# A two-layer decoder trunk: every fourth weight chunk gets its low part from an accumulating DMA instead of VectorE

## The chip, the cores and the metric

The kernel runs on one core of one Trainium2 chip. The metric is the device time of one execution in microseconds. Two runs of the kernel before took 2312.23 and 2313.69 us, median 2312.96. The engines are called as in the profile: PE is TensorE's matmul, PEld its weight load, DVE VectorE, ACT ScalarE, POOL GpSimd, SP SyncE, which here only issues DMAs.

## The reference

A sequence of 256 tokens with 2048 features in float32 passes two layers. Each layer is a token mixer, a layer norm of `ALPHA * x + mixer(x)`, a gated feed-forward net with a short causal convolution, and a layer norm again. Layer 0 mixes by a gated linear recurrence (HGRN2), layer 1 by causal spatial gating (gMLP).

```python
def hgrn2_mixer(x, w_in, norm_g, w_out, lb):      # layer 0
    q, f, i, g = split(x @ w_in, 4)               # 2048 -> 4 x 2048
    ...                                           # recurrence over the tokens, 16 heads
    return (rms_norm(o) * norm_g * silu(g)) @ w_out

def chunked_gmlp(x, w_in, ln_g, ln_b, w_s, b_s, w_out):   # layer 1
    u, v = split(gelu(x @ w_in), 2)               # 2048 -> 2 x 2048
    ...                                           # v normed, mixed over tokens in chunks of 128
    return (u * gate) @ w_out

def conv_ffn(x, w_up, conv_w, conv_b, w_down):    # both layers
    a, b = split(x @ w_up, 2)                     # 2048 -> 2 x 5632
    a = causal_conv3(a, conv_w) + conv_b
    return (silu(a) * b) @ w_down                 # 5632 -> 2048

for layer in range(2):
    h = layer_norm(ALPHA * h + mixer[layer](h))
    h = layer_norm(ALPHA * h + conv_ffn(h))
```

Nearly all the work is in the products with weights. There are 392 blocks of 512 x 512 weights, each read once from HBM.

## The kernel before, in words

**Exact sums of two parts.** [...] The kernel keeps float32 accuracy by writing each operand as hi + lo, where hi is the value rounded to float32r and lo is what is left, and computes hi*hi + hi*lo + lo*hi. Activations X and Y are kept so for all 256 tokens. Weights are split as they arrive.

**Chunks.** A chunk is a 512 x 512 block of a weight matrix, [128, 4, 512] on chip, 1 MiB. `plan` lists all chunks in the order in which the products take them; `want` appends, with `extra=True` for six that use buffers of a pool of their own. `fetch` issues the DMA of the next chunk into a `raw` tile, on SP's queue. `convert` makes the tiles `hi` (named whi in the profile) and `lo` (wlo): in two pieces of 1024 columns, ACT copies raw to hi (L83), which rounds it, and DVE subtracts hi from raw into lo (L84). `chunk` is called by a product when it takes a chunk; it first calls `ahead(AHEAD)`, with AHEAD = 3, so that the fetch and the conversion of the next two chunks stand in the program ahead of the products of this one. raw, hi and lo have three buffers each (pool `wp`, `bufs=3`).

**Products.** In `block_b` the weights are stationary and the output has the features on the partitions: a block of 512 output features takes four chunks, each with 16 pairs of matmuls, L149 (hi times both parts of the activations) and L156 (lo times their high part). In `block_a` the activations are stationary (L113 hi, L114 lo, L115 hi): each chunk has 24 matmuls. Both need the low part in their first two instructions of a chunk. PE runs the chunks one after another in the order of the plan.

**Stages.** HGRN2: four groups of three `block_b`, one `block_a` and the recurrence, then the output product. FFN: the features go in groups of 3, 4 and 4 blocks of 512, each block two `block_b` (up) and, after each group, four `block_a` (down). gMLP: four `block_a` for v, four `block_b` for u with the gating, four `block_a` out. Then the FFN of layer 1.

**Order.** The instructions are recorded in program order and a scheduler orders them on each engine's queue by readiness as it reckons it; each engine then works its queue in order. On a queue an instruction that waits holds up what stands behind it. POOL's queue in the kernel before holds constants and, later, broadcasts: rows of layer-norm vectors (`g`, `b`, `gb`, `bb`, L314) and gMLP's biases and mixing weights (`bs` L685, `wsT` L655). `residual` applies a layer norm's gain and bias to z, ordered behind the last L84 recorded (`self.last_lo`).

Of the kernel before, what the change touches and what calls it, by code (L numbers as in the profile page):

```python
# [8 lines left out]
F32 = mybir.dt.float32  # L9
F32R = mybir.dt.float32r  # L10
U32 = mybir.dt.uint32
AF = mybir.ActivationFunctionType
ALU = mybir.AluOpType
# [20 lines left out]


class Trunk:
    """Activations that feed products are kept as an exact sum of two float32r parts,
    feature on the partition, [P, k, part, token]; weights are split the same way as
    they arrive, and a product is hi*hi + hi*lo + lo*hi."""

    def __init__(self, ctx, tc, a):
        self.tc = tc
        self.nc = nc = tc.nc
        self.a = a
        self.ctx = ctx
        ent = ctx.enter_context
        self.cp = ent(tc.tile_pool(name="cp", bufs=1))
        self.wp = ent(tc.tile_pool(name="wp", bufs=3))
        self.acc = ent(tc.tile_pool(name="acc", bufs=6, space=PSUM))
        self.misc = ent(tc.tile_pool(name="misc", bufs=2, space=PSUM))  # L50
        cp = self.cp
        self.X = cp.tile([P, NK, 2, S], F32R, name="X")
        self.Y = cp.tile([P, NK, 2, S], F32R, name="Y")
        self.z = cp.tile([P, 2, D], F32, name="z")
        self.small = ent(tc.tile_pool(name="small", bufs=2))
        self.plan = []
        self.issued = 0
        self.taken = 0
        self.ready = []

    # ---------------------------------------------------------------- weights
    def want(self, w, k0, c0, extra=False):
        self.plan.append((w, k0, c0, extra))

# [10 lines left out]
    def convert(self, raw, extra, pieces=2):  # L75
        nc = self.nc
        pool = self.xp if extra else self.wp
        hi = pool.tile([P, CK, NB], F32R, tag="hi", name="whi")
        lo = pool.tile([P, CK, NB], F32R, tag="lo", name="wlo")
        n = CK // pieces  # L80
        for i in range(0, CK, n):
            s = slice(i, i + n)
            nc.scalar.copy(hi[:, s, :], raw[:, s, :])  # L83
            self.last_lo = nc.vector.tensor_tensor(  # L84
                lo[:, s, :], raw[:, s, :], hi[:, s, :].bitcast(F32), ALU.subtract
            )
        self.ready.append((hi, lo))
# [8 lines left out]
        self.taken += 1  # L96
        return self.ready.pop(0)

    # ---------------------------------------------------------------- products
    def block_a(self, act, ka, w, k0, nch, c0, evac, staggered=False, halves=False):  # L100
        """out[token, c0:c0+NB]; act is stationary."""
        nc = self.nc
        ps = [self.acc.tile([P, NB], F32, tag="acc", name="pa") for _ in range(2)]
        n = [0, 0]

        def part(ch, ci, t):
            hi, lo = ch
            for kk in range(CK):
                k = ka + ci * CK + kk
                xh = act[:, k, 0, t * P : (t + 1) * P]  # L110
                xl = act[:, k, 1, t * P : (t + 1) * P]
                last = n[t] == nch * CK - 1
                nc.tensor.matmul(ps[t], xh, hi[:, kk, :], start=n[t] == 0, stop=False)  # L113
                nc.tensor.matmul(ps[t], xh, lo[:, kk, :], start=False, stop=False)  # L114
                nc.tensor.matmul(ps[t], xl, hi[:, kk, :], start=False, stop=last)  # L115
                n[t] += 1

        take = lambda ci: self.chunk(w, k0 + ci * CK, c0)
        first = max(0, nch - 4) if staggered else nch
        head = []  # L120
        if halves:
            head = [take(ci) for ci in range(min(3, nch))]
            for t in range(2):
                for ci, ch in enumerate(head):
                    part(ch, ci, t)
        for ci in range(len(head), first):
            ch = take(ci)
            for t in range(2):
                part(ch, ci, t)
        held = [take(ci) for ci in range(first, nch)]  # L130
        for t in range(2):
            for i, ch in enumerate(held):
                part(ch, first + i, t)
            if held:
                evac(t, ps[t])
        if not held:
            for t in range(2):
                evac(t, ps[t])

    def block_b(self, act, w, nch, c0, evac, halves=False):  # L140
        """out[c0 + feature, token] in four tiles, [P, main | rest, token]; the weights
        are stationary."""
        nc = self.nc
        ps = [self.acc.tile([P, 2, S], F32, tag="acc", name="pb") for _ in range(4)]
        last = nch * CK - 1
# [42 lines left out]
            evac(j, ps[j])  # L188

    def gather(self, pool, ps, out):  # L190
        """out = main + rest of a tile of block_b."""
        nc = self.nc
        r = pool.tile([P, S], F32, tag="rest", name="rest")
        nc.scalar.copy(r, ps[:, 1, :])  # L194
        nc.vector.tensor_tensor(out, ps[:, 0, :], r, ALU.add)

    def split(self, out, k, src):
        """out[:, k] = the two parts of src [P, token]."""
        nc = self.nc
        nc.scalar.copy(out[:, k, 0, :], src)  # L200
        nc.vector.tensor_tensor(
            out[:, k, 1, :], src, out[:, k, 0, :].bitcast(F32), ALU.subtract
        )

    # ---------------------------------------------------------------- constants
    def load_x(self, k0, n):
        x = self.a["x"][0].rearrange("(t p) d -> p t d", p=P)
        s = slice(k0 * P, (k0 + n) * P)
# [8 lines left out]
        nc.gpsimd.memset(self.eps[:, 1:2], RMS_EPS)  # L217

    def load_vectors(self, rows_sb):
        """Per-feature vectors as columns: feature k*P + p of row r at [p, base + k]."""  # L220
        nc, cp, a = self.nc, self.cp, self.a
        rows = []
        self.rows = []
# [45 lines left out]
        return self.cols[:, b + k : b + k + n]  # L269

    def bounds(self, h1):
        """lb = softmax over the rows of lb_logits, row 0, and 1 - lb."""
        nc, cp = self.nc, self.cp
        t = h1.tile([P, 6, NK], F32, tag="sg", name="lbt")
        m, e, rest, tot = t[:, 0, :], t[:, 1:4, :], t[:, 4, :], t[:, 5, :]
# [9 lines left out]
        nc.vector.tensor_tensor(self.lb[:, 0, :], e[:, 0, :], tot, ALU.mult)  # L285
        nc.vector.tensor_tensor(self.lb[:, 1, :], rest, tot, ALU.mult)

    # ---------------------------------------------------------------- layouts
    def turn(self, t, k0, n=4, g=None, b=None):
        """X[:, k0 : k0 + n, :, half t] from the columns of z[half t], with x -> g*x + b."""  # L290
        nc = self.nc
        ps = self.misc.tile([P, n, P], F32, tag="m", name="pt")
        for j in range(n):
# [14 lines left out]
            self.X[:, k0 : k0 + n, 1, s], src, hi.bitcast(F32), ALU.subtract  # L308
        )

    # ---------------------------------------------------------------- layer norm
    def broadcast(self, pool, ap, c, tag, **kw):
        r = pool.tile([P, NB], F32, tag=tag, name=tag, **kw)
        self.nc.gpsimd.dma_start(  # L314
# [10 lines left out]
        return mv  # L325

    def norm(self, name, l, store=None):
        """Layer norm of z, half by half as its last product arrives. With store, the
        result goes there; without, it goes to X, and z holds it once residual() has run."""
        nc = self.nc  # L330
        g, b = self.a[name + "_g"][l], self.a[name + "_b"][l]
        self.ln = ExitStack()
# [38 lines left out]
            self.ln.close()  # L371

    def add_z(self, c, first=False, last=False):
        """evac of block_a: z[:, t, NB columns c] gains the product, the first time as
        ALPHA * z + product."""
        nc = self.nc

        def evac(t, ps):
            with self.tc.high_priority() if last else nullcontext():
                step(t, ps)  # L380

        def step(t, ps):
            zz = self.z[:, t, c * NB : (c + 1) * NB]
            if first:
                nc.vector.scalar_tensor_tensor(zz, zz, ALPHA, ps, ALU.mult, ALU.add)
            else:
                nc.vector.tensor_tensor(zz, zz, ps, ALU.add)  # L387
            if last:
                nc.vector.bn_stats(self.stats[t][:, c, :], zz)
                if c == 3:  # L390
                    self.after_stats(t)

        return evac

    # ---------------------------------------------------------------- HGRN2
    def plan_hgrn(self):
        w, wo = self.a["hg_w_in"][0], self.a["hg_w_out"][0]
        for g in range(4):
# [7 lines left out]
            self.want(wo, 3 * CK, c * NB, c == 3)  # L406

    def masks(self):
        """mask[b][s, (group, i, r)] = 1 where row s lies in segment i of that group of four
        segments of b rows."""  # L410
        nc, cp = self.nc, self.cp
        self.mask = {}
        for b in LEVELS:
# [98 lines left out]
                self.split(self.Y, h, y.rearrange("p t n -> p (t n)"))  # L512

    def mix(self, q, f, k1, v, sc, o, ss, lp, h1):
        """Two heads. The decay between s < t is a product of forget gates; it is taken as
        (gates from s to the end of its segment) * (gates of the segments between) *
        (gates from the start of t's segment), at the one level of a division of the tokens
        by four at which s and t part. Q and K carry the outer two."""
        nc = self.nc
        flat = lambda x: x.rearrange("p h n -> p (h n)")  # L520
        own = lambda th: slice((th % 2 * 2 + th // 2) * P, (th % 2 * 2 + th // 2 + 1) * P)
# [95 lines left out]
        self.staggered_pass(self.Y, 12, wo, 12)  # L617

    def staggered_pass(self, act, ka, w, k0):
        """The last CK k-tiles of all four column blocks, half t = 0 first."""  # L620
        nc = self.nc
        ev = [self.add_z(c, last=True) for c in range(4)]
        held = [self.chunk(w, k0, c * NB) for c in range(4)]
# [9 lines left out]
                    nc.tensor.matmul(ps, xl, hi[:, kk, :], start=False, stop=kk == CK - 1)  # L633
                ev[c](t, ps)

    # ---------------------------------------------------------------- gMLP
    def plan_gmlp(self):
        w, wo = self.a["sg_w_in"][0], self.a["sg_w_out"][0]
        for part in (1, 0):
# [84 lines left out]
            self.block_a(self.Y, 0, a["sg_w_out"][0], 0, 4, c * NB,  # L724
                         self.add_z(c, first=True, last=True), staggered=c == 3)

    # ---------------------------------------------------------------- ConvFFN
    def plan_ffn(self, l):
        up, down = self.a["ffn_w_up"][l], self.a["ffn_w_down"][l]
        m = 0  # L730
# [125 lines left out]
```

## Time and profile before

| what | value |
|---|---|
| median of two runs | 2312.96 us (2312.23 to 2313.69) |
| span of the profiled execution | 2310.0 us |
| granted PE clock, mean | 0.998 |
| PE busy | 2287.9 us, 99% |
| DVE busy | 1499.2 us, 65% |
| ACT busy | 1090.2 us, 47% |
| POOL busy | 43.3 us, 2% |
| HBM read | 425.98 MB, 185 GB/s over the span |

The profile is of one execution; its span is from the first instruction to the last, and 3 us lie between it and the median of the runs. A group's row gives the line, the engine, the operation, the tiles written and read, the shapes, the count, then the busy time and the mean duration of one in ns, then the idle time of the engine just ahead and what ended it. A row of the timeline gives the start, the duration of what is merged in it, the engine and the operation, and in brackets the idle time before it. Matmuls are pipelined and their ends modelled.

### The profile page before, as it was taken

Reading aid. Unit: us, or ns where it says so; the run is one execution under the profiler, and the core shown is the slowest. Engines: PE = TensorE matmul, PEld = TensorE weight load, DVE = VectorE, ACT = ScalarE, POOL = GpSimd, SP = SyncE. Lnnn points to the kernel's source line nnn. Section 1 sums busy time; section 2 is a strip of 40 time slices with the busy share of each in tenths; the row PEclk is TensorE's granted clock in tenths of the full one; section 3 lists DMA queues with packets and bytes.
Section 4 is the critical chain, followed back from the end, with each engine's and each line's share of the span. In section 5 each row is a group of like instructions: output and inputs, shape, how many; then the busy total and the mean of one; then the engine's idle time right before and its main releaser. Section 6 shows DMA issues by size and latency. Waiting matters only on the chain.

```text
span 2310.0 us, 30477 instructions
## 1 busy us (share of the span) xinstructions
PE 2287.9 (99%) x12141; PEld 1956.5 (85%) x12141; DVE 1499.2 (65%) x2407; ACT 1090.2 (47%) x1642; POOL 43.3 (2%) x86
## 2 busy tenths in 40 slices
PE   8999999999999999999999999999999999999998
PEld 7888888888888888888888888888888888888886
DVE  5868786857765666456665776566765566466656
ACT  5565555536443444334443645445443444344442
POOL 2000000000000000000000000000000000000000
PEclk9999999999999999999999999999999999999999
DMA  7454535464466555555555676655565555555553
GB/s 257 129 185 137 187 134 185 146 234 158 170 214 218 188 183 182 200 182 187 191 189 182 201 223 192 214 181 178 189 228 182 193 183 189 194 189 183 182 198 112
DMA packets 214046, 430.05 MB, mean 186 GB/s; under 512 B 7544, under 2 KB 8336, under 8 KB 213904
## 3 DMA queue, kind: packets, MB, share of 16 engines
q1 hardware_dynamic: 209536, 415.26, 53.2%
q0 software_dynamic: 4368, 12.85, 1.9%
q8 instruction: 95, 1.56, 0.3%
q14 instruction: 47, 0.39, 0.0%
HBM read 425.98 MB, written 2.10 MB: 185 GB/s over the span
## 4 chain that ended last, share of the span: by engine, by line
PE 96%; DVE 2%; DMA 1%; ACT 0%; SPq 0%; issue 0%; DVEq 0%; ACTq 0%
PE pb L149 38%; PE pb L156 19%; PE pa L115 12%; PE pa L114 12%; PE pa L113 12%; PE pl L544 1%; DMA z<-in_x_dram 1%; DVE wlo L84 0%; PE pt L295 0%; DVE scores L553 0%; PE pg L710 0%; PE pa L632 0%; PE pa L633 0%; PE pa L631 0%; PE pl L577 0%; DVE K L559 0%
## 5 line engine op out<-in xcount | busy, mean ns | idle before, releaser
L84 DVE TENSOR_TENSOR wlo<-raw,whi 128x1024 fp32r<-128x1024 f32 (+1 forms) x786 | 929.4, 1218 | 683.5 <-ACT whi L83 675.6
L149 PE MATMUL pb<-X,whi 128*128 128x512 f32 (+1 forms) x3960 | 1348.8, 391 | 1.9 <-DVE X L307 1.9
L83 ACT CAST whi<-raw 128x1024 fp32r<-128x1024 f32 (+1 forms) x786 | 789.5, 1047 | 911.9 <-PE pb L149 435.3
L156 PE MATMUL pb<-X,wlo 128*128 128x256 f32 x3840 | 1054.5, 282 | 0.0
L149 PEld LDWEIGHTS pb<-X,whi 128*128 128x128 f32 x3960 | 726.5, 188 | 166.9 <-DVE X L307 2.4
L156 PEld LDWEIGHTS pb<-X,wlo 128*128 128x128 f32 x3840 | 713.1, 188 | 4.9
L115 PE MATMUL pa<-whi,Y 128*128 128x512 f32 x928 | 365.1, 393 | 0.0
L114 PE MATMUL pa<-wlo,Y 128*128 128x512 f32 x928 | 364.6, 393 | 0.0
L113 PE MATMUL pa<-whi,Y 128*128 128x512 f32 x928 | 361.3, 389 | 0.0
L114 PEld LDWEIGHTS pa<-wlo,Y 128*128 128x128 f32 x928 | 174.3, 188 | 39.6
L113 PEld LDWEIGHTS pa<-whi,Y 128*128 128x128 f32 x928 | 174.2, 188 | 38.8
L115 PEld LDWEIGHTS pa<-whi,Y 128*128 128x128 f32 x928 | 174.5, 188 | 35.3
L194 ACT COPY rest<-pb 128x256 f32<-128x256 f32 x240 | 87.3, 369 | 115.6 <-PE pb L149 112.3
L115 PE MATMUL pa<-whi,X 128*128 128x512 f32 x256 | 100.7, 393 | 0.0
L113 PE MATMUL pa<-whi,X 128*128 128x512 f32 x256 | 100.3, 392 | 0.0
L114 PE MATMUL pa<-wlo,X 128*128 128x512 f32 x256 | 100.2, 392 | 0.0
L761 DVE SCALAR_TENSOR_TENSOR act<-a,cols,act 128x254 f32<-128x254 f32 (+1 forms) x176 | 73.1, 477 | 0.0
L114 PEld LDWEIGHTS pa<-wlo,X 128*128 128x128 f32 x256 | 48.1, 188 | 10.8
L115 PEld LDWEIGHTS pa<-whi,X 128*128 128x128 f32 x256 | 48.1, 188 | 10.2
L113 PEld LDWEIGHTS pa<-whi,X 128*128 128x128 f32 x256 | 48.1, 188 | 10.0
L387 DVE TENSOR_TENSOR z<-z,pa 128x512 f32<-128x512 f32 x40 | 27.4, 684 | 34.3 <-PE pa L115 30.1
L553 DVE COPY_PREDICATED scores<-mask,pl 128x192 f32<-128x192 uint32 (+2 forms) x144 | 40.9, 354 | 2.0 <-PE pl L544 1.8
(161 smaller groups left out, 1082.0 us busy)
## 6 DMA issues: line engine op xcount, KB each, us to landing
raw<-in_ffn_w_up_dram SPq DMA_DIRECT2D x176, 1024.0 KB, 4.9
raw<-in_ffn_w_down_dram SPq DMA_DIRECT2D x88, 1024.0 KB, 5.1
raw<-in_hg_w_in_dram SPq DMA_DIRECT2D x63, 1024.0 KB, 5.1
raw<-in_sg_w_in_dram SPq DMA_DIRECT2D x32, 1024.0 KB, 5.5
raw<-in_hg_w_out_dram SPq DMA_DIRECT2D x16, 1024.0 KB, 5.1
raw<-in_sg_w_out_dram SPq DMA_DIRECT2D x16, 1024.0 KB, 5.1
g<-in_ln_g_dram POOLq DMA_DIRECT2D x16, 256.0 KB, 5.9
b<-in_ln_b_dram POOLq DMA_DIRECT2D x16, 256.0 KB, 8.7
```

The lines of the kernel that those rows point to most:

```text
L83: nc.scalar.copy(hi[:, s, :], raw[:, s, :])
L84: self.last_lo = nc.vector.tensor_tensor(lo[:, s, :], raw[:, s, :], hi[:, s, :].bitcast(F32), ALU.subtract)
L113: nc.tensor.matmul(ps[t], xh, hi[:, kk, :], start=n[t] == 0, stop=False)
L114: nc.tensor.matmul(ps[t], xh, lo[:, kk, :], start=False, stop=False)
L115: nc.tensor.matmul(ps[t], xl, hi[:, kk, :], start=False, stop=last)
L149: nc.tensor.matmul(ps[j][:, :, s], ch[0][:, k % CK, c], act[:, k, :, s], start=start and k == 0, stop=k == last, skip_group_check=halves,)
L156: nc.tensor.matmul(ps[j][:, 1, :], ch[1][:, k % CK, c], act[:, k, 0, :], start=False, stop=False, skip_group_check=halves,)
L194: nc.scalar.copy(r, ps[:, 1, :])
L387: nc.vector.tensor_tensor(zz, zz, ps, ALU.add)
L544: nc.tensor.matmul(pl[:, h, :], K[:, own(2 * t + h)], W[:, 2 * h + t, :], start=True, stop=True)
L553: nc.vector.copy_predicated(dst, mk.unsqueeze(1).to_broadcast([P, 2, P // 4 // b, w]), src)
L761: nc.vector.scalar_tensor_tensor(cv[:, d:], x[:, : S - d], self.c(("cw", l, 2 - d), f), cv[:, d:], ALU.mult, ALU.add,)
```

## The change

A counter in `convert` numbers the chunks in the order in which they are converted. From chunk 16 on, every fourth that isn't one of the extra ones is converted in another way: ACT copies raw to hi in one piece of 2048 columns, ACT writes -hi to lo, and a DMA issued by POOL adds raw onto lo. The result is the same, raw - hi. The other chunks keep the two pieces on ACT and DVE. `self.last_lo` is set by these alone. Docstrings and comment lines are emptied, so that line numbers after `convert` are 8 higher (L83 and L84 of other chunks are now L91 and L92).

```diff
@@ __init__
         self.taken = 0
+        self.formed = 0
         self.ready = []
@@ convert
         hi = pool.tile([P, CK, NB], F32R, tag="hi", name="whi")
         lo = pool.tile([P, CK, NB], F32R, tag="lo", name="wlo")
+        self.formed += 1
+        if self.formed > 12 and self.formed % 4 == 0 and not extra:
+            nc.scalar.copy(hi, raw)
+            nc.scalar.activation(lo, hi.bitcast(F32), AF.Copy, scale=-1.0)
+            nc.gpsimd.dma_start(lo, raw, accum_op=ALU.add)
+            self.ready.append((hi, lo))
+            return
         n = CK // pieces
...
```

ACT's queue in the FFN of layer 0, at the end of one feature block and the beginning of the next. Before (L83 is the cast to hi, L194 and L200 evacuate and split a product, L765 is the silu):

```order
L83 CAST whi<-raw 128x1024 x2
L200 CAST Y<-b 128x256 x2
L83 CAST whi<-raw 128x1024 x6
L194 COPY rest<-pb 128x256 x4
L83 CAST whi<-raw 128x1024
```

The same place with the change (lines 8 higher but for the new L83 and L84):

```order
L91 CAST whi<-raw 128x1024 x2
L208 CAST Y<-b 128x256 x2
L83 CAST whi<-raw 128x2048
L84 ACTIVATE wlo<-whi 128x2048
L91 CAST whi<-raw 128x1024 x4
L202 COPY rest<-pb 128x256 x4
L91 CAST whi<-raw 128x1024
```

Of three chunks cast in a row, the first now has one cast of double width, and the negation stands right behind it, ahead of the casts of the next two.

POOL's queue from the last blocks of gMLP's gating to its output product. Before (bs are biases, g and b the vectors of the next layer norm):

```order
L685 DMA bs<-in_sg_b_s_dram 128x512 x3
L314 DMA g_12413<-in_ln_g_dram 128x512
L314 DMA g_12415<-in_ln_g_dram 128x512
L314 DMA g_12417<-in_ln_g_dram 128x512
L314 DMA g_12419<-in_ln_g_dram 128x512
L314 DMA b_12421<-in_ln_b_dram 128x512
```

With the change (L85 is the accumulating DMA; the one ahead of the g rows is chunk 244's, the first behind the b rows chunk 248's):

```order
L85 DMA wlo<-raw 128x2048
L693 DMA bs<-in_sg_b_s_dram 128x512
L85 DMA wlo<-raw 128x2048
L322 DMA g_12358<-in_ln_g_dram 128x512
L322 DMA g_12360<-in_ln_g_dram 128x512
L322 DMA g_12362<-in_ln_g_dram 128x512
L322 DMA g_12364<-in_ln_g_dram 128x512
L322 DMA b_12366<-in_ln_b_dram 128x512
L322 DMA b_12368<-in_ln_b_dram 128x512
L322 DMA b_12370<-in_ln_b_dram 128x512
L322 DMA b_12372<-in_ln_b_dram 128x512
L85 DMA wlo<-raw 128x2048 x8
```

The broadcasts, which stood alone on this queue, now have accumulating DMAs between them, and the eight of the layer norm stand together ahead of chunk 248's.

## The prediction

> **What bounds the kernel now.** I read the page first: busy time, then the chain that ended last and the costliest groups.
>
> ```profile
> span 2310.0 us, 30477 instructions
> PE 2287.9 (99%) x12141; PEld 1956.5 (85%) x12141; DVE 1499.2 (65%) x2407; ACT 1090.2 (47%) x1642; POOL 43.3 (2%) x86
> ...
> PE 96%; DVE 2%; DMA 1%; ACT 0%; SPq 0%; issue 0%; DVEq 0%; ACTq 0%
> ...
> L84 DVE TENSOR_TENSOR wlo<-raw,whi 128x1024 fp32r<-128x1024 f32 (+1 forms) x786 | 929.4, 1218 | 683.5 <-ACT whi L83 675.6
> ...
> L83 ACT CAST whi<-raw 128x1024 fp32r<-128x1024 f32 (+1 forms) x786 | 789.5, 1047 | 911.9 <-PE pb L149 435.3
> ```
>
> TensorE is the bound and carries 96% of the chain. VectorE, which the change relieves, is on 2% of it and spends 683.5 us idle just ahead of L84, waiting for the high part. The windows view tells how much of TensorE's time could be won (columns: length, PE busy, PEld, DVE, ACT, POOL, granted clock, DMA share, GB/s), and the list of waits says what PE waited for.
>
> ```profile
> core 0: us, PE busy (x) PEld busy (x) DVE busy (x) ACT busy (x) POOL busy (x), PEclk, DMA share, GB/s
> ...
> 20.00:2290.00 2270.00, 2266.80 (x12041) 1939.25 (x12040) 1475.98 (x2371) 1078.82 (x1623) 27.07 (x50) 1.00 0.55 186
> 2290.00:2310.00 20.00, 9.85 (x43) 7.70 (x41) 13.08 (x23) 0.59 (x2) 0.00 (x0) 0.81 0.28 105
> ```
> ```profile
> PE pt L295 <- DMA z<-in_x_dram: 8.8, 4, 3.9
> PE pb L149 <- DVE X L307: 1.9, 2, 1.1
> PE pv L264 <- DVE cols L265: 0.5, 1, 0.5
> ```
>
> Between 20 and 2290 us PE is idle for 2270.00 - 2266.80 = 3.2 us, and no wait of PE names a weight tile. So the weights always come in time, and taking work off VectorE can win some 3 us at most. The question is whether a low part made by DMA still comes in time.
>
> **The time that a low part has.** The same stretch on three queues, ACT, DVE and SP, in the steady part of the first FFN:
>
> ```profile
> 1103.08 2.00 ACT L83 CAST whi<-raw 128x1024 fp32r<-128x1024 f32 x2 [2.70 <-PE pb L149]
> 1108.74 2.00 ACT L83 CAST whi<-raw 128x1024 fp32r<-128x1024 f32 x2 [3.65 <-PE pb L149]
> 1114.43 2.00 ACT L83 CAST whi<-raw 128x1024 fp32r<-128x1024 f32 x2 [3.69 <-issue]
> ```
> ```profile
> 1104.16 2.36 DVE L84 TENSOR_TENSOR wlo<-raw,whi 128x1024 fp32r<-128x1024 f32 x2 [2.16 <-ACT whi L83]
> 1109.82 2.36 DVE L84 TENSOR_TENSOR wlo<-raw,whi 128x1024 fp32r<-128x1024 f32 x2 [3.29 <-ACT whi L83]
> ```
> ```profile
> 1106.55 0.37 SPq L72 DMA_DIRECT2D raw<-in_ffn_w_up_dram  x1
> ```
>
> A chunk is converted the moment that PE has done with the chunk three before it, since there are three buffers for each part: the cast at 1103.08 waited for PE, for nothing else. PE then consumes two more chunks and needs this one when the next-but-one cast starts, at 1114.43: 11.35 us later. Today the low part is there at 1104.16 + 2.36 = 1106.52, and 1106.55 is the next fetch into the freed raw buffer. Nearly 8 us are spare.
>
> **The change, part by part.** It removes two L84 instructions for each chosen chunk. The plan has 392 chunks; every fourth from number 16 on makes 95, six of which are the extras, so 89: 178 x 1.22 = 217 us of VectorE, all of it under PE's 2266.80 us. Worth to the end: 0 (bound above: the 3.2 us).
>
> It adds to ScalarE a 2048-wide negation and makes one 2048-wide cast of two 1024-wide. Durations, by shape:
>
> ```profile
> L83 ACT CAST whi<-raw 128x1024 fp32r<-128x1024 f32 x782 | 787.2, 1049 | 911.9 <-PE pb L149 435.3 <-PE pa L115 354.9 <-issue 95.1
> ...
> L83 ACT CAST whi<-raw 128x512 fp32r<-128x512 f32 x4 | 2.3, 621 | 0.0
> ```
>
> 512 more columns cost 0.43 us, so 2048 cost 1.05 + 0.86 = 1.9 us; with the pair's 2.00 I take 2.0 for each of the two. ScalarE gains 89 x 2.0 = 178 us on 1090, nowhere near the bound. But for the chosen chunk the two are in series ahead of the transfer: 4.0 of its 11.35 us. Three hand-overs (ACT to ACT, ACT to POOL, landing to PE) take a little more: DVE follows ACT in the rows above by 1104.16 - 1103.08 - 1.05 = 0.03 us; I allow 0.35 in all for queues that sleep longer. **The transfer has about 7.0 us from its issue on POOL to its landing.**
>
> No accumulating transfer is in the trace. Its neighbours:
>
> ```profile
> q1 hardware_dynamic: 209536, 415.26, 53.2%
> q0 software_dynamic: 4368, 12.85, 1.9%
> ...
> raw<-in_ffn_w_up_dram SPq DMA_DIRECT2D x176, 1024.0 KB, 4.9
> ...
> g<-in_ln_g_dram POOLq DMA_DIRECT2D x16, 256.0 KB, 5.9
> b<-in_ln_b_dram POOLq DMA_DIRECT2D x16, 256.0 KB, 8.7
> ...
> wsT<-in_sg_w_s_dram POOLq DMA_DIRECT2D x1, 1024.0 KB, 9.5
> bs<-in_sg_b_s_dram POOLq DMA_DIRECT2D x4, 256.0 KB, 3.7
> ```
>
> Packets of q1 took 53.2% of 16 x 2310 us for 415.26 MB: 21.1 GB/s an engine, 338 GB/s together. 1024 KB (1.049 MB) is 3.1 us at that rate, so a fetch has 4.9 - 3.1 = 1.8 us around its data. POOL's queue q0: 12.85 MB in 1.9% is 293 GB/s; 256 KB is 0.9 us, and the single broadcast bs has 3.7 - 0.9 = 2.8 us around it. An accumulating transfer has to read the raw chunk and the negated one, 2.097 MB.
> - Low end: the second read costs nothing and POOL no more than SP, 4.9 us, no stall.
> - High end by these rows: both reads in turn at q0's rate, 7.2 + 2.8 = 10.0 us. wsT, the one transfer of this size that POOL issues, took 9.5 with a single read, though in rows of 512 bytes.
> - I take both reads in turn at the fetch's rate, 6.2, and 2.3 around them (between 1.8 and 2.8): **8.5 us, 1.5 over.** It is nearest to wsT among the rows for this queue, without its short rows.
>
> Other traffic is little in its way: the raw buffer is held until the sum has landed, so the fetch that today starts at 1106.55 waits for it, and the one before it (5.65 us earlier, 4.9 long) has landed by then. That later fetch is covered: it has until PE has done with the chosen chunk, another 5.65 us, for its 4.9. If it slipped, it would cost the difference each time.
>
> The collectives page of the Trainium skill (Collectives: The Full Stack, the section on the bandwidth ceiling) says that a reducing transfer runs at half a copy's speed, because it reads two sources through one ring, and the add is free. No row here shows one; it agrees with doubling the data term.
>
> 89 x 1.5 = 134 us.
>
> POOL's queue is the second cost. Its order now mixes the sums with broadcasts that wait for buffers:
>
> ```profile
> 679.59 2.23 POOL L314 DMA_DIRECT2D g<-in_ln_g_dram  x4 [222.37 <-DVE z L369]
> ...
> 1379.45 1.20 POOL L314 DMA_DIRECT2D bb<-in_sg_ln_b_dram  x2 [2.72 <-DVE v L703]
> ...
> 1472.94 2.12 POOL L314 DMA_DIRECT2D g<-in_ln_g_dram  x4 [26.41 <-DVE Y L201]
> 1475.05 2.12 POOL L314 DMA_DIRECT2D b<-in_ln_b_dram  x4
> ```
> ```profile
> 1472.99 2.00 ACT L83 CAST whi<-raw 128x1024 fp32r<-128x1024 f32 x2 [1.71 <-PE pa L115]
> ```
>
> The worst place is chunk 248, cast at 1472.99: eight broadcasts stand ahead of its sum, the last issued at about 1476.6 and landed 8.7 later, at 1485.3. With 6.2 us of data behind that, the sum lands at 1491.5, against a need at 1472.99 + 11.3 = 1484.3: 7.2 late, 6 more than the usual. At 679.59 (chunk 108, three broadcasts ahead), at its twin in layer 1 and at 1379.45 (chunk 232) the same reckoning gives about 2 each. Together 12 us. Who waits is always PE.
>
> Sum: 2310.0 + 134 + 12 = 2456 us of span; the runs' median, 2312.96, lies 3 us above the span, so **2458 us**.
>
> **The rivals.**
> *The sum lands in time.* If the two reads overlap, or cost less in SBUF than from memory, the transfer takes under 7.0 us and PE never waits, apart from the 12 us of POOL's order: 2313 to 2325 us. For it: 7.0 us is 2.1 more than a fetch of the same bytes takes. Against it: POOL's transfers show 2.8 us around the data. Up to 7.3 us the loss stays within 2% (89 x 0.3 + 12 = 39 us), which is also about what a measurement of this kernel can tell from no change. The Trainium skill's page DMA: Bandwidth & Descriptors, on the anatomy of a transfer issued by GpSimd, fits 2.0 us + bytes / 436 GB/s; as an estimate, 2.097 MB would take 6.8 us and the time would be this rival's. The trace disagrees for bs: 2.6 by the fit, 3.7 measured. Chance 0.26.
>
> *The adder is slow.* Nothing here bounds the rate at which a transfer adds. At 13 us the stall is 6.0, 89 x 6.0 + 12 = 546, and the time 2859 us. It gets worse if PE's clock falls in long waits: the only place where it is below 1.00 above is the end, 0.81 with PE half idle. TensorE: Matmul & The Clock Gate, Part 1, in the Trainium skill, states that the clock halves after an idle window of about 3.4 us; no wait of PE in this trace's middle is that long. Stalls of 1.5 us would escape that rule, stalls of 6 would not. For this rival: wsT's 9.5. Chance 0.16 for over 10.4 us.
>
> *VectorE was a hidden brake.* It would need PE idle that a wait on wlo ends. There is none, and 3.2 us are all that can be won: 2310. Chance of over 2% faster: 0.02.
>
> **How the numbers follow.** The forecast's group (transfer 7.3 to 10.4 us, time 2359 to 2630) has 0.56, the rival in time 0.26, the slow adder 0.16, faster 0.02. Slower is 0.56 + 0.16 = 0.72, same 0.26. The range starts inside the rival in time, 2318, leaving about 0.05 below it. Its top is beyond the high end of the rows (10.0 us: 89 x 3.0 + 12 = 279, 2592), because an adder has no row: 11.2 us gives 89 x 4.2 + 12 = 386, 2700, with 0.13 above.
>
> **What would show it.** In the changed profile: L92 (the old L84) on DVE with 608 instructions; a new ACT row of 89 negations near 1.9 us, and 89 more transfers of 1024 KB in the list of issues, whose median to landing is the number all hangs on (8.5). PE's waits should name the accumulating DMA some 89 times, about 1.5 us each, and PE's busy time should stay at 2288. I am wrong if that wait is missing (the landing is then under 7.0), if the landing is over 10.4, if PE waits on the high part or a raw fetch instead, or if matmuls get slower.

## The result and the profile after

The changed kernel took 2428.78 us (2426.87 and 2430.70), against 2312.96 us before: a ratio of 1.0502, 95% interval 1.0485 to 1.0519. It is 116 us slower, on the side and within the range of the prediction, which named 2458. The sum behind that number was right in its frame and wrong in the sizes of its two terms, one too large and one too small, and it put other traffic at nothing; that the total came near is in part luck, as the experiments show.

The page of the changed kernel, and its windows view (the columns as before):

```profile
span 2429.0 us, 30514 instructions
PE 2329.4 (96%) x12141; PEld 1967.7 (81%) x12141; DVE 1297.1 (53%) x2229; ACT 1251.0 (52%) x1642; POOL 118.0 (5%) x175
...
q0 software_dynamic: 17184, 106.18, 21.2%
...
PE 52%; DMA 20%; issue 4%; ACT 1%; DVE 1%; POOLq 0%; DVEq 0%; POOL 0%; ACTq 0%
...
L92 DVE TENSOR_TENSOR wlo<-raw,whi 128x1024 fp32r<-128x1024 f32 (+1 forms) x608 | 718.4, 1217 | 880.2 <-ACT whi L91 872.8
...
L85 POOL DMA_DIRECT2D wlo<-raw x89 | 75.4, 848 | 2060.3 <-ACT wlo L84 1627.7
L84 ACT ACTIVATE wlo<-whi 128x2048 fp32r<-128x2048 f32 x89 | 170.6, 1917 | 2.4
...
wlo<-raw POOLq DMA_DIRECT2D x89, 1024.0 KB, 7.4
```
```profile
20.00:2405.00 2385.00, 2305.24 (x12035) 1947.52 (x12034) 1274.87 (x2194) 1241.20 (x1625) 102.88 (x141) 0.99 0.71 216
```

VectorE lost 929.4 - 718.4 = 211 us of subtractions, and nothing was won by it. The accumulating DMA, which stands at 20% of the chain, is what PE now waits for. The list of PE's waits in the changed kernel (us in total, times, the longest):

```profile
PE pa L122 <- DMA wlo<-raw: 43.3, 32, 6.1
PE pb L164 <- DMA wlo<-raw: 32.9, 34, 3.1
```

The time went to three places. In the middle of the run PE is idle for 2385.00 - 2305.24 = 79.8 us instead of 3.2, which is 76.6 more, and the two rows above name 76.2 of it. PE's busy time grew by 2329.4 - 2287.9 = 41.5 us for the same matmuls. Part of that is a slower clock, 0.989 in the mean instead of 0.998: 0.011 x 2429 - 0.002 x 2310 = 22 us. The rest lies at the waits themselves: the matmul before a wait is drawn to its end, and the one after it takes 0.38 us where its like takes 0.28 (below). Together 118 of 119 us of span.

One of the chosen chunks in the steady part of the first FFN, on ACT, POOL and PE:

```profile
1177.16 1.91 ACT L83 CAST whi<-raw 128x2048 fp32r<-128x2048 f32 x1 [1.70 <-PE pb L157]
1179.10 1.92 ACT L84 ACTIVATE wlo<-whi 128x2048 fp32r<-128x2048 f32 x1
```
```profile
1181.31 0.84 POOL L85 DMA_DIRECT2D wlo<-raw  x1 [21.82 <-ACT wlo L84]
```
```profile
1188.03 0.40 PE L157 MATMUL pb<-X,whi 128*128 128x512 f32 x1
1188.66 0.38 PE L164 MATMUL pb<-X,wlo 128*128 128x256 f32 x1 [0.24 <-DMA wlo<-raw]
1188.89 0.39 PE L157 MATMUL pb<-X,whi 128*128 128x512 f32 x1
```

Cast, negation, issue: 4.15 us from the beginning of the cast, as forecast. PE takes the low part at 1188.66, which is 7.35 us after the issue; without a wait it would have come 0.24 us behind its predecessor, at 1188.27. So this sum is 0.4 us late, not 1.5.

Worked out in this way from the starts of the first matmul of each of the 89 low parts: 18 come in time, 44 are late by under 1 us (22 us together), 13 by 1 to 2 us (18 us), 14 by more (48 us). The typical wait is small. The tail is over half of the sum of 88 us.

### The profile page after: what moved, and what is told of

The parts are those of the page before. It is cut to its first block, busy times and chain, and to the rows that moved or that the text cites. A ratio compares the mean times of both kernels' runs of the same rounds, so it can differ in the third digit from the quotient of the medians.

```text
span 2429.0 us, 30514 instructions
## 1 busy us (share of the span) xinstructions
PE 2329.4 (96%) x12141; PEld 1967.7 (81%) x12141; DVE 1297.1 (53%) x2229; ACT 1251.0 (52%) x1642; POOL 118.0 (5%) x175
## 4 chain that ended last, share of the span: by engine, by line
PE 52%; DMA 20%; issue 4%; ACT 1%; DVE 1%; POOLq 0%; DVEq 0%; POOL 0%; ACTq 0%
PE pb L157 21%; DMA wlo<-raw 20%; PE pb L164 11%; PE pa L122 7%; PE pa L123 6%; PE pa L121 6%; ACT wlo L84 0%; ACT whi L83 0%; PE pg L718 0%; PE pt L303 0%; ACT turn L310 0%; DVE wlo L92 0%; PE pa L639 0%; PE pa L641 0%; PE pa L640 0%
## 5 line engine op out<-in xcount | busy, mean ns | idle before, releaser
L92 DVE TENSOR_TENSOR wlo<-raw,whi 128x1024 fp32r<-128x1024 f32 (+1 forms) x608 | 718.4, 1217 | 880.2 <-ACT whi L91 872.8
L91 ACT CAST whi<-raw 128x1024 fp32r<-128x1024 f32 (+1 forms) x608 | 610.0, 1046 | 612.4 <-PE pb L157 296.5
L83 ACT CAST whi<-raw 128x2048 fp32r<-128x2048 f32 x89 | 170.0, 1910 | 206.9 <-PE pb L157 117.8
L85 POOL DMA_DIRECT2D wlo<-raw x89 | 75.4, 848 | 2060.3 <-ACT wlo L84 1627.7
L84 ACT ACTIVATE wlo<-whi 128x2048 fp32r<-128x2048 f32 x89 | 170.6, 1917 | 2.4
L121 PEld LDWEIGHTS pa<-whi,X 128*128 128x128 f32 x256 | 49.0, 192 | 10.9 <-ACT whi L91 0.2
```

What stands on the lines that cost most here:

```text
L83: nc.scalar.copy(hi, raw)
L84: nc.scalar.activation(lo, hi.bitcast(F32), AF.Copy, scale=-1.0)
L85: nc.gpsimd.dma_start(lo, raw, accum_op=ALU.add)
L92: self.last_lo = nc.vector.tensor_tensor(lo[:, s, :], raw[:, s, :], hi[:, s, :].bitcast(F32), ALU.subtract)
```

## The experiments

Theory A, from the prediction: the loss is lead time, since cast, negation and a transfer that reads two sources in turn take longer than the 11.1 us that the buffers allow. Theory B, the rival: the loss is the price of the added traffic, of raw buffers held longer and of POOL's queue, whatever waits for the sums. The first four kernels tell these apart, the last four divide the loss. The kernel before ran beside each four: 2312.57 and 2312.84 us.

**The transfer without a product that waits for it.**

```diff
-            nc.scalar.copy(hi, raw)
-            nc.scalar.activation(lo, hi.bitcast(F32), AF.Copy, scale=-1.0)
-            nc.gpsimd.dma_start(lo, raw, accum_op=ALU.add)
+            for i in range(0, CK, 2):
+                ...   # cut: cast and subtraction of one half, as in the kernel before
+            nc.gpsimd.dma_start(raw, raw, accum_op=ALU.add)
```

> The same 89 chunks are converted as in the kernel before (two casts on ScalarE, two subtractions on VectorE), and POOL then adds raw onto raw itself by an accumulating DMA whose result nobody reads: two reads and one write of 1 MiB as in the change, the raw buffer held until it lands, POOL's queue with 89 more entries, but no product waits for it. Theory A (lead time): 2313 to 2320 us. Rival B (traffic, held raw buffers, POOL's queue): most of the 116 us stays, 2400 us or more.

2319.4 us, ratio 1.003 (1.0018 to 1.0042). The transfers are as long as in the change (the page's issues: KB each, median us from the issue to the landing):

```profile
raw<-raw POOLq DMA_DIRECT2D x89, 1024.0 KB, 7.4
```

No wait of PE names them. Of the 116 us, 7 are the price of traffic and of POOL's queue by themselves; the largest new wait of PE is one of 4.0 us on VectorE in gMLP's gating. Theory B falls. Traffic still does something where a product waits, as the later runs show.

**A plain copy in place of the sum.**

```diff
-            nc.gpsimd.dma_start(lo, raw, accum_op=ALU.add)
+            nc.gpsimd.dma_start(lo, raw)
```

> The 89 transfers are plain copies of raw onto lo, without the addition (the low part of these chunks is left out of the product). Everything else, the negation included, stays. Theory A (lead time: the sum lands 7.4 us after its issue where 7.0 are to be had, because it reads two sources one after the other): with one read the 5.2 us of packets become 2.6, the copy lands after 1.4 + 2.6 + 0.4 = 4.4 us, PE waits for it only where POOL's broadcasts stand ahead, and the time is 2315 to 2330 us. Rival B (the loss is the price of 89 MB more traffic and of POOL's software queue, whatever is read): 89 MB are still written, landing stays near 7, the time stays within 1% of 2429 us.

2334.0 us, ratio 1.0091 (1.0076 to 1.0106), 4 us beyond the expected range.

```profile
wlo<-raw POOLq DMA_DIRECT2D x89, 1024.0 KB, 4.3
```

The same queue, bytes written and order, one read less: 4.3 us instead of 7.4, as expected (4.4). What remains is at the places where the transfer doesn't run alone: PE still waits for it six times, 13.1 us in all, the longest 3.9, and four falls of PE's clock in the middle of the run follow.

**One negation more ahead of the sum.**

```diff
             nc.scalar.activation(lo, hi.bitcast(F32), AF.Copy, scale=-1.0)
+            nc.scalar.activation(lo, hi.bitcast(F32), AF.Copy, scale=-1.0)
```

> ScalarE writes the negation twice, so that the accumulating DMA starts 1.9 us later; traffic and POOL's queue are the same. Theory A: each of 89 chunks is 1.9 us later, 170 us more, and PE's clock falls after more of the waits, which now are 2 to 3 us long: 2600 to 2650 us. Rival B (traffic): ScalarE has room (1251 of 2429 us busy), at most 2435 us.

2737.8 us, ratio 1.1849 (1.183 to 1.1869): 88 us above the range expected by A, and ScalarE was busy 52% of the span. The waits of PE, the issues, and then four stretches around one wait in the windows view:

```profile
PE pb L165 <- DMA wlo<-raw: 153.8, 52, 3.8
PE pa L123 <- DMA wlo<-raw: 125.8, 33, 11.3
```
```profile
wlo<-raw POOLq DMA_DIRECT2D x89, 1024.0 KB, 8.0
```
```profile
1176.00:1179.40 3.40, 3.40 (x21) 2.93 (x20) 0.00 (x0) 2.66 (x2) 0.00 (x0) 1.00 0.85 299
1188.00:1191.00 3.00, 0.14 (x1) 0.14 (x2) 1.91 (x2) 1.99 (x2) 0.00 (x0) 1.00 1.00 205
1191.00:1194.40 3.40, 3.40 (x12) 2.92 (x13) 0.70 (x2) 0.37 (x1) 0.00 (x0) 0.50 1.04 397
1194.40:1197.80 3.40, 3.40 (x21) 2.95 (x21) 2.06 (x7) 0.75 (x2) 0.00 (x0) 1.00 1.05 392
```

Two things were missing from the expectation. A wait on pb is 3.0 us in the mean, where 0.4 + 1.9 would be 2.3, since the later sum also meets the next raw fetch: in the steady part SP issues it 3.1 us after the sum, and its packets come in among the sum's last ones (8.0 to landing). And PE's clock: in the second window PE is idle, in the third it is busy throughout at a granted clock of 0.50 and gets 12 matmuls done where the fourth has 21. Nine matmuls fewer in a stretch are some 1.6 us. In the middle of the run the clock records have 70 such stretches, of 3.4 us or two or three times that, 280 us in all: at half speed about 140 us. With the 280 us of the two rows that is 420; the span grew by 422.

**Negation first, straight from raw.**

```diff
-            nc.scalar.copy(hi, raw)
-            nc.scalar.activation(lo, hi.bitcast(F32), AF.Copy, scale=-1.0)
+            nc.scalar.activation(lo, raw, AF.Copy, scale=-1.0)
             nc.gpsimd.dma_start(lo, raw, accum_op=ALU.add)
+            nc.scalar.copy(hi, raw)
```

> ScalarE writes -raw, rounded, to lo straight from raw, ahead of the cast to hi; rounding is symmetric, so lo is -hi as before, and the accumulating DMA no longer has the cast ahead of it. It is issued 1.9 us earlier. Theory A: a typical sum, now 0.4 us late, is 1.5 us early; only the places with broadcasts ahead of the sum on POOL's queue stay late (6 us become 4 at three places, and a few of 1 us), some with a fall of PE's clock: 2330 to 2345 us. Rival B (traffic): nothing changes, 2429 us.

2365.2 us, ratio 1.023 (1.0215 to 1.0246). Taking 1.9 us out of the chain gives back 64 of 116 us, by theory A's mechanism, but 20 us less than expected. The sums now take longer:

```profile
wlo<-raw POOLq DMA_DIRECT2D x89, 1024.0 KB, 7.8
```
```profile
PE pa L122 <- DMA wlo<-raw: 21.6, 6, 5.4
...
PE pb L164 <- DMA wlo<-raw: 8.8, 7, 3.4
```

Issued 2 us earlier, many sums meet a raw fetch that in the change was over by then: of the 42 in the up products of the two FFNs, 22 send their first packet later than 1.8 us after the issue, 2.4 in the median, instead of 1.4; in the change two do. Of the 53 us that remain, 30 are 13 waits, the long ones among them; PE's clock falls behind six of them.

**Fewer sums.**

```diff
-        if self.formed > 12 and self.formed % 4 == 0 and not extra:
+        if self.formed > 12 and self.formed % 8 == 0 and not extra:
```

> Every eighth chunk instead of every fourth, from 16 on: 46 of the 89 sums (those of 88, 104, 216, 232, 248 and 288 among them; the late ones at 100, 108, 228, 280 are gone). If each sum pays for itself (typical wait 0.45 us, and long waits where POOL's broadcasts, a raw fetch or an instruction fetch stand in the way), half of the typical loss and about half of the long waits remain: 2350 to 2375 us. If the loss is one of throughput that appears only beyond some rate of sums, it falls by far more than half: under 2325.

2366.5 us, ratio 1.0231 (1.0215 to 1.0246); there are 45 sums, not the 46 that the expectation counted. Half of the sums cost 54 of 116 us: between these two rates they pay one by one, and nothing shows a rate beyond which the loss would begin.

**The sums behind broadcasts left out.**

```diff
-        if self.formed > 12 and self.formed % 4 == 0 and not extra:
+        if (self.formed > 12 and self.formed % 4 == 0 and not extra
+                and self.formed not in (68, 108, 228, 232, 248, 288)):
```

> Every fourth chunk as in the change but for six that are left to VectorE: 68, 108, 228, 232, 248, 288, the sums that stand behind broadcasts on POOL's queue. Theory: these places cost 6.2, 5.3, 4.7 and 5.8 us of waiting (108, 228, 248, 288) and about 1.7 us of halved clock for each 3.4 us window that follows, some 22 + 8 = 30 us in all: 2395 to 2405 us. Rival: another sum takes their place behind the broadcasts and the time stays within 5 us of 2429.

2389.4 us, ratio 1.033 (1.0314 to 1.0345): 39 us less than the change, 6 to 16 more than expected. No other sum takes their place. Six sums of 89 make a third of the loss. How one of them waits is seen at chunk 108 of the changed kernel, on POOL's and SP's timelines and in PE's waits and windows of the same stretch:

```profile
713.57 1.67 POOL L322 DMA_DIRECT2D g<-in_ln_g_dram  x3 [21.04 <-DVE z L377]
716.48 0.87 POOL L85 DMA_DIRECT2D wlo<-raw  x1 [1.25 <-ACT wlo L84]
```
```profile
715.60 0.37 SPq L73 DMA_DIRECT2D raw<-in_ffn_w_down_dram  x1
```
```profile
PE pa L122 <- DMA wlo<-raw: 6.1, 1, 6.1
```
```profile
726.60:733.40 6.80, 3.84 (x9) 3.07 (x10) 1.01 (x1) 0.00 (x0) 0.00 (x0) 0.50 1.02 370
733.40:740.20 6.80, 6.80 (x30) 5.52 (x30) 2.10 (x2) 2.00 (x2) 0.00 (x0) 1.00 0.80 296
```

The sum is issued on time, 4.2 us after its cast, but three broadcasts of 256 KB and a raw fetch, issued 0.9 us before it, are still under way. By the DMA packets the broadcasts run until 2 us after the sum's issue, and its own first packet goes out at 4.8 us, when the raw fetch thins out. It is 6 us late, and PE's clock is halved for 6.8 us, in 3.8 of which PE works. Chunk 288, the twin in layer 1, has the same raw fetch in the way, so the 39 us are the price of these six places and not of broadcasts alone; the two were not tried apart.

**Two half sums.**

```diff
-            nc.scalar.copy(hi, raw)
-            nc.scalar.activation(lo, hi.bitcast(F32), AF.Copy, scale=-1.0)
-            nc.gpsimd.dma_start(lo, raw, accum_op=ALU.add)
+            for i in range(0, CK, 2):
+                s = slice(i, i + 2)
+                nc.scalar.copy(hi[:, s, :], raw[:, s, :])
+                nc.scalar.activation(lo[:, s, :], hi[:, s, :].bitcast(F32), AF.Copy, scale=-1.0)
+                nc.gpsimd.dma_start(lo[:, s, :], raw[:, s, :], accum_op=ALU.add)
```

> Cast, negation and sum in two halves of 1024 columns: the first half's sum is issued 2.1 us after the buffer is free, the second's at about 4.3 us with half the data. Theory of lead time: the second lands after 1.4 + 2.6 + 0.4 us if the first is out of its way, at 8.8 to 9.5 us of the 11.1, so only the places behind broadcasts remain: 2335 to 2365 us. Rival: each transfer issued by POOL pays its fixed part and the two stand behind each other, landing as late as one: 2420 us or more.

2355.4 us, ratio 1.0187 (1.017 to 1.0204), as expected. Twice as many transfers, and still 73 us less: what counts is when the last byte lands. Waits for the sums are down to 28.4 us in 20.

**Both repairs.** Negation first, and the six sums left to VectorE (the two diffs above).

> Negation straight from raw ahead of the cast, and the six chunks behind broadcasts left to VectorE. What remains is the long wait at chunks 100 and 280 (a raw fetch in the way, 3 us each with the fall of the clock some 5) and a few of under 1 us: 2320 to 2332 us. If the two repairs mend the same waits, it is no better than negation first alone, 2365.

2336.0 us, ratio 1.0099 (1.0084 to 1.0114), 4 us above the range. The two give 64 and 39 us alone and 93 together, so they mend mostly different waits. What is left, by PE's waits and their longest:

```profile
PE pb L165 <- DMA wlo<-raw: 8.2, 7, 3.5
...
PE pa L123 <- DMA wlo<-raw: 1.7, 1, 1.7
```

The long ones are at chunks 100 and 280, as expected. No version beats the kernel before. In the middle of the run none that only converts weights in another way could win more than the 3.2 us for which PE is idle there.

## Why the prediction held

**The bound: right.** PE was the limit, VectorE's work was hidden, and 211 us less of it moved nothing.

**The lead: right.** Forecast 7.0 us from issue to landing. In the up products a sum that lands 6.9 us after its issue is just in time, one of 7.3 is 0.4 late (chunk 188). 18 sums are in time, four of them in HGRN with 10 us to spare.

**The transfer: right mechanism, mis-sized.** "Both reads in turn at the fetch's rate, 6.2, and 2.3 around them: 8.5" was 7.4 in the median and 6.9 at the least. The packets of an undisturbed sum say where: 128 of 8 KB, eight for each engine, 0.644 us each, so 5.15 us of data; the first goes out 1.41 us after the issue and the landing is 0.3 behind the last. Two reads in turn it is, as the plain copy shows (0.33 us for a packet of the same size, 4.3 to landing), but at 25.4 GB/s an engine instead of 21.1, and with less around them than the broadcast bs suggested. With 7.4 the term of 134 us would have been 89 x 0.4 = 36. The sign that the prediction named, some 89 waits of 1.5 us, came as 66 of 1.2 in the mean. Of the Trainium skill's pages that were weighed, the fit in DMA: Bandwidth & Descriptors (the anatomy of a transfer issued by GpSimd; 6.8 us as an estimate) is within 0.1 of an undisturbed sum, nearer than the reckoning from rows, though the time was not that rival's: 6.9 is for a sum alone, and most are not alone. The half speed that the Trainium skill states for a reducing transfer (Collectives: The Full Stack, the section on the bandwidth ceiling) agrees too: 0.644 us a packet against 0.33.

**Other traffic: wrong.** The prediction put it at nothing ("Other traffic is little in its way"). But a sum alone, at 6.9 us, is just in time, and what else the DMA engines carry makes it late. By the DMA packets of the changed kernel, 23 of the 42 sums in the up products have a 16 KB packet of the instruction queue beside them that starts within 1.2 us of the issue; they land at 7.5 us in the median, while ten of the other 19 land at 6.9. Chunk 188 above is one of the 23. In the down products the next raw fetch is issued some 4.8 us after the sum and meets its last packets: 7.2 in the median. The 14 waits of over 2 us divide the same way: an instruction packet at the end (chunks 88, 92, 96, 104, 244; 12 us together), a raw fetch ahead (100, 280; 6 us), broadcasts ahead, at all but 248 with a raw fetch too (108, 228, 248, 288; 22 us), and a raw fetch that comes in early, 3.1 to 3.5 us after the sum's issue (72, 216, 256; 8 us; with one negation more, 3.1 us is the rule and 8.0 the landing). This is read from the trace; of these causes only the places behind broadcasts were taken away by an experiment.

**POOL's order: right place, mis-sized.** Forecast 12 us; leaving the six sums out won 39. The long waits were at 108, 228, 248 and 288 (some 5 to 6 us each), not at 232, and neither the raw fetch in the way nor the price of the clock behind them was in the term.

**The clock: in the wrong case.** The prediction had its fall in the slow rival alone: "stalls of 1.5 us would escape that rule, stalls of 6 would not". A wait of 2.2 us was enough at chunk 96, one of 2.6 at chunk 72 was not. What decides is where the wait lies: the stretches at half speed all begin on a grid of 3.413 us that is fixed within a run, and the windows view, laid on that grid, shows chunk 72 in its first two rows and chunk 96 in the last two:

```profile
494.48:497.89 3.41, 1.58 (x7) 0.94 (x6) 0.95 (x1) 1.99 (x2) 0.00 (x0) 1.00 0.97 147
497.89:501.31 3.42, 2.77 (x12) 2.31 (x13) 1.41 (x2) 0.00 (x0) 0.00 (x0) 1.00 1.03 384
644.66:648.08 3.42, 1.41 (x9) 0.99 (x8) 1.51 (x2) 1.99 (x2) 0.00 (x0) 1.00 0.02 5
648.08:651.49 3.41, 3.41 (x13) 2.92 (x12) 1.28 (x2) 0.38 (x1) 0.00 (x0) 0.50 0.82 261
```

At chunk 72 the wait is divided between two cells of the grid, 1.83 and 0.65 us of idle PE, and the clock stays; at chunk 96 one cell has 2.01 us, and the next runs at 0.50. The Trainium skill's page TensorE: Matmul & The Clock Gate, Part 1, speaks of an idle window of about 3.4 us; here a window idle for 2.0 of its 3.4 us was enough. The falls made 22 of the 116 us, and with them came a part of the prediction's own sign of being wrong, "if matmuls get slower".

So the sum, 134 + 12, has the composition wrong. Measured, some 40 us are in 57 waits of under 2 us, 48 in the 14 longer ones and 22 in the clock. That 2458 lies within 30 us of 2429 is in part luck: a transfer reckoned 1.1 us too long stood in for other traffic and for the clock, which were not in the sum. A prediction with the right transfer and its own 12 us would have read 2361 us, at the edge of no difference. Two slips in its sums change nothing: 2310 + 134 + 12 and the 3 us are 2459, and a transfer of 7.3 us gives 2352, where it writes 2359, which is the line of 2%.

**The rivals.** In time: 18 sums of 89 were. The slow adder: no, an undisturbed sum needs no more than its two reads. Theory B's 7 us are real but small. VectorE as a hidden brake: excluded.

## What to carry to other kernels

Moving work off an engine that is not the bound buys nothing, and the path it takes instead has to be timed against the lead that the buffers give, not against its throughput: here a chain without slack, late by 0.4 us at a typical place and by 2 to 6 us at fourteen, cost 5%. If a transfer must be waited for, shorten what stands ahead of it (order, a dependence that isn't one, halves), and look at the queue that issues it for transfers that wait for other things. A wait of TensorE of about 2 us and more can cost its length and, for each 3.4 us at half clock behind it, up to 1.7 us again.

## What the runs showed of the hardware that was not expected

- An accumulating DMA within SBUF of 1 MiB, raw onto lo, lands 6.9 us after its issue when nothing else moves, a plain copy on the same queue 4.1 (the least of 89 each).
- PE's granted clock falls to 0.50 in stretches of one or more cells of a 3.413 us grid, fixed within a run. In the ten profiles, away from the ends, 6733 cells were at full clock: 106 were followed by half speed, with PE, as the profile draws it, idle in each for 1.83 us or more, and in none of the other 6627 was it idle for over 1.87 us. With a wait of some 3 us at nearly every fourth chunk (one negation more) there were 70 such stretches in 2732 us.
- A transfer that POOL issues 0.6 or 1.0 us after a 1 MiB fetch by SP sends its first packet only when the fetch is mostly through: 3.1 us (chunk 100, issued 1.0 us behind) and 4.4 us (chunk 280, 0.6) after its issue instead of 1.4.
- At chunks 88, 92, 96, 104 and 244 the sum landed 2 us later than its neighbours, and in each of these a packet of 16 KB of the instruction queue was on one of the DMA engines at its end. Read from the DMA packets of chunk 92 (us after the issue; the trace doesn't name the engine, the shares are told apart by packets that follow one another):

```text
15 engines: last data packet ends by 6.61, semaphore packet by 6.6
1 engine:   last data packet ends at 7.13
            instruction packet, 16 KB, from 7.11 to 8.04
            semaphore packet at 8.03
PE goes on at 9.19 (neighbours: 0.4 after the last data packet)
```

One late share of sixteen holds up the whole sum. That the instruction packet is the cause was seen in five places and not tried by an experiment, and such a packet at the end is not always enough: at chunks 332 and 380 the sum landed at 7.9 beside one; why PE goes on only 1.1 us after the last semaphore packet stays open.
